# The last normed tile's splits, the place of M4 and the last pair's down weights in a hybrid decoder layer's FFN

## The chip, the cores and the metric

One Trainium2 chip, one NeuronCore of it. The number that counts is the device time of one execution in microseconds (us), the median of several. All engines are named as the profile names them: PE is the matrix engine, DVE the vector engine, ACT the scalar engine, POOL GpSimd, SP the engine that issues the DMAs here.

## What is computed

One decoder layer on x[1, 1024, 1024] in float32, cut to the lines that matter here:

```python
mod = silu(c) @ w_ada + b_ada                      # shift1, scale1, gate1, shift2, scale2, gate2
h = rmsnorm(x, norm1_w) * (1 + scale1) + shift1
proj = h @ w_in                                    # queries, keys, index heads, retention, gates
y_a = dsa_attention(...) @ w_attn_proj             # top-256 index search, then attention
y_r = (silu(gr) * head_groupnorm(retention)) @ w_ret_proj
merged = sigmoid(ga) * y_a + sigmoid(gb) * y_r
x = x + gate1 * (merged @ w_out)
h2 = rmsnorm(x, norm2_w) * (1 + scale2) + shift2
ffn = (silu(h2 @ w_ffn_gate) * (h2 @ w_ffn_up)) @ w_ffn_down    # 2816 hidden columns
x = x + gate2 * ffn
return rmsnorm(x, final_norm_w)
```

## The kernel before

Every matrix product is made from float32 operands that are split into a high part (ACT rounds it) and a low part (the rest, a subtraction on DVE or POOL). A product of two 128x128 blocks then takes three matmuls: high by high, high by low, low by high.

The change touches the last two of the kernel's stages, the end of the out-projection with it.

**End of the out-projection.** For each of eight tiles of 128 tokens the second half of `merged @ w_out` is added to x, its norm is taken, the normed tile is turned on PE (line 1394), and scaled by ACT (L1400) and DVE (L1404) into `hraw`. The eight tiles go in the order 4, 5, 6, 7, 0, 1, 2, 3. The first four are the token half "2", the last four the token half "1". `put_half1` and `put_rest` make side operands of the scaled tiles with `put_combo`, which is one ACT instruction (L1294, the high part) and one DVE instruction (L1295, the low part): h11 is the first half of the channels of the token half 1, h21 its second half.

**Gate and up projection of the FFN.** The 2816 hidden columns are 11 pairs p = 0 ... 10 of 256; each pair is two streams, one on `w_ffn_gate` and one on `w_ffn_up`, so there are 22 streams. A stream is a 2x2 block product (token halves and channel halves against channel halves and column halves) made in seven block products instead of eight: `M1` to `M7`. The side operands of the seven are made once: h11 for M1, h21 for M2, h22 for M4, S1 for M5, S2 for M6, S4 for M3, S3 for M7 (`split_combo` makes S2, S4 and S3, ACT L1519 and DVE L1520). The other operand of a product, its factor, is a sum of blocks of the stream's weights (DVE L800, L806, L807; M1, M2 and M3 need no sum), split by `split_block` into `fhi` (ACT L761) and `flo` (L762; DVE for the first products, POOL afterwards, by `fenv.lo_engine`). There are five buffers for fhi and flo each. A product is 12 matmuls of 128x128 by 128x512: four blocks of k, each with L838 (high, high), L840 (high, low side) and L842 (low factor, high side). Products add up in two PSUM tiles of a stream: M1, M6, M7 and M4 in its tile `ya`, M5 and M3 in its tile `yb`, M2 in a `yb` of its own. Between them ACT copies (L818) and DVE adds (L821) take partial sums out of these into `c11`, `c12`, `c21`, `c22`; DVE adds and multiplies (L1448) and ACT silus (L1445) finish them. `finish_tasks(p)` puts the pair's seven left operands of the down product on a list: DVE sums, then stores to `act_d` in DRAM by `act_store`, then the loading of down weights (`down_load`, into the tile `dw`) and their sums (`down_sums`, DVE L1502) and the store of these to `dw_d` in DRAM. Two of these tasks are taken off after each product.

**Order.** The list `seq` names (stream, product) in the order in which the program issues them: the first two streams product by product, then stream after stream in `ORDER = M1, M5, M6, M3, M7, M2, M4`. A scheduler then places each engine's instructions; `turns_after(ins, other)` asks it to keep one instruction behind another, without a wait of its own. Every engine works through its own queue in order.

**Down product.** The same seven products, each summed over the 11 pairs: `down_slot` loads a 128x512 block from `act_d`, `dw_d` or `w_ffn_down` into a ring of eight (`draw`), and splits it (ACT L1603; DVE or POOL L1604) into a `dslot`. The products go M1, M5, M6, M3, M7, M4 and M2; PE runs them at L1621 to L1623. At the end the final norm is applied, with `fnorm`.

Of the kernel before, what the change touches and what calls it, by code (L numbers as in the profile page):

```python
# [43 lines left out]
def tile_hybrid_layer(ctx: ExitStack, tc: tile.TileContext, x, c, w_ada, b_ada, norm1_w, w_in,  # L44
# [715 lines left out]
    def split_block(src, hi, lo, eng=None):  # L760
        ins = nc.scalar.activation(hi, src, AF.Copy)  # L761
        (eng or nc.gpsimd).tensor_sub(lo, src, f32(hi))  # L762
        return ins

    class Stream:
# [28 lines left out]
        def factor(self, m):  # L794
# [18 lines left out]
            self.split = split_block(src, hi, lo, self.env.lo_engine)  # L813
# [70 lines left out]
    class GateEnv:  # L884
# [423 lines left out]
    def put_half1(o):  # L1308

        h11, h21, h12, s1 = parts_of(o)  # L1310
        put_combo("h11", o, h11)
        nc.vector.tensor_sub(s1, s1, h11)

    def put_rest(o):

        h11, h21, h12, s2 = parts_of(o)
        put_combo("h21", o, h21)
        nc.vector.tensor_sub(h21, h21, s2)

# [28 lines left out]
    for hf in range(2):  # L1348
# [16 lines left out]
        for n, t in enumerate(order):  # L1365
# [130 lines left out]
    def down_sums(p):  # L1496
# [16 lines left out]
        todo.insert(4, lambda: nc.sync.dma_start(out=dw_d[p], in_=dws[p]))  # L1513

    def split_combo(name, srcs):
        alloc_combo(name)
        for k in range(4):
            hi, lo = (c[:, k, :] for c in combo[name])
            nc.scalar.activation(hi, srcs[:, k, :], AF.Copy)  # L1519
            nc.vector.tensor_sub(lo, srcs[:, k, :], f32(hi))  # L1520
# [13 lines left out]
    for st in flow[:2]:  # L1534
        st.prepare("M1")
        turns_after(scaled[3], st.split)
    s3 = ffn.tile([P, 4, H], F32, name="s3", tag="dw")
    held2 = const.tile([P, 2, H], F32, name="held2", tag="gate")

    for st, after in zip(flow, (None, {0: 2}, {2: 3}, {0: 3})):  # L1540
        st.product("M5", after)
        if st.p == 0:
            turns_after(scaled[3], st.copied)
    split_combo("S2", hraw[1][:, 1])
# [3 lines left out]

    def behind(i):
        st, m = seq[i]  # L1550
        if i == 0:
            for k in range(4):
                nc.vector.tensor_sub(s3[:, k, :], hraw[0][:, 0, k, :], hraw[1][:, 0, k, :])
        if i == 1:
# [3 lines left out]
        if i == 8:  # L1558
            fenv.lo_engine = nc.gpsimd
        if i == 9:  # L1560
# [30 lines left out]
    fnorm = ffn.tile([P, 4, H], F32, name="fnorm", tag="dw")[:, 0:2, :].rearrange("p a n -> p (a n)")  # L1591
    nc.sync.dma_start(out=fnorm, in_=final_norm_w.rearrange("(o d) -> o d", o=1).partition_broadcast(P))
# [163 lines left out]
```

## Time and profile before

| what | us |
|---|---|
| time, median of 3 runs | 1771.59 (1771.57 to 1774.38) |
| the profiled execution's own time | 1770.31 |
| its span, first to last instruction | 1768.4 |
| PE busy in the span | 1696.3 (96%) |
| DVE, POOL, ACT busy | 1216.7 (69%), 882.4 (50%), 757.2 (43%) |
| mean granted clock of PE | 0.991 |

The span is the time from the first to the last instruction on the core. A full granted clock is 1.00. Of PE's busy time the page says that matmuls are pipelined, so the start-to-start distance of neighbouring matmuls says more than their durations.

### The profile page before, as it was taken

Reading aid. Unit: us, or ns where it says so; the run is one execution under the profiler, and the core shown is the slowest. Engines: PE = TensorE matmul, PEld = TensorE weight load, DVE = VectorE, ACT = ScalarE, POOL = GpSimd, SP = SyncE. Lnnn points to the kernel's source line nnn. Section 1 sums busy time; section 2 is a strip of 40 time slices with the busy share of each in tenths; the row PEclk is TensorE's granted clock in tenths of the full one; section 3 lists DMA queues with packets and bytes.
Section 4 is the critical chain, followed back from the end, with each engine's and each line's share of the span. In section 5 each row is a group of like instructions: output and inputs, shape, how many; then the busy total and the mean of one; then the engine's idle time right before and its main releaser. Section 6 shows DMA issues by size and latency. Waiting matters only on the chain. (4 is left out here: it accounts for less than half of the span.)

```text
span 1768.4 us, 24625 instructions
## 1 busy us (share of the span) xinstructions
PE 1696.3 (96%) x8266; PEld 1393.6 (79%) x8266; DVE 1216.7 (69%) x2099; ACT 757.2 (43%) x1469; POOL 882.4 (50%) x873
## 2 busy tenths in 40 slices
PE   5899989999999999999999999899999999999998
PEld 4797768888878887788777888688787778787887
DVE  7529793888998687574675747865756565686665
ACT  3625533333544444430676146533333333444444
POOL 3563275683544678430355631054544445556564
PEclk9999999999999999999999999999999999999999
DMA  9535452512333355964843720134444444597762
GB/s 276 161 99 169 149 162 62 149 39 57 117 90 131 112 172 176 291 182 146 196 116 136 244 98 1 54 107 165 158 156 160 137 150 143 203 320 247 209 183 107
DMA packets 182654, 266.48 MB, mean 151 GB/s; under 512 B 13872, under 2 KB 111616, under 8 KB 180096
## 3 DMA queue, kind: packets, MB, share of 16 engines
q1 hardware_dynamic: 182528, 264.91, 48.1%
q8 instruction: 65, 1.06, 0.3%
q14 instruction: 61, 0.50, 0.1%
HBM read 195.39 MB, written 69.47 MB: 150 GB/s over the span
## 5 line engine op out<-in xcount | busy, mean ns | idle before, releaser
L80 POOL TENSOR_TENSOR wlo<-wraw,whi 128x512 fp32r<-128x512 f32 (+2 forms) x116 | 147.0, 1279 | 105.3 <-ACT whi L77 86.3
L463 DVE TENSOR_SCALAR_CACHE_REDUCE eq<-score,cand 128x384 uint8<-128x384 f32 (+2 forms) x192 | 180.5, 940 | 3.6
L762 POOL TENSOR_TENSOR flo<-tmp,fhi 128x512 fp32r<-128x512 f32 x79 | 107.1, 1356 | 139.7 <-ACT fhi L761 111.8
L121 PE MATMUL mm<-whi,hT_hi 128*128 128x512 f32 (+1 forms) x432 | 159.8, 376 | 3.8 <-ACT qk L650 1.8
L124 PE MATMUL mm<-whi,hT_lo 128*128 128x512 f32 (+1 forms) x432 | 161.5, 376 | 0.0
L123 PE MATMUL mm<-wlo,hT_hi 128*128 128x512 f32 (+1 forms) x432 | 160.3, 374 | 0.0
L838 PE MATMUL ya<-hc,fhi 128*128 128x512 f32 x344 | 134.6, 392 | 2.3 <-DVE c L821 1.4
L1604 DVE TENSOR_TENSOR dslot<-draw,dslot 128x512 fp32r<-128x512 f32 x88 | 94.7, 1107 | 58.4 <-ACT dslot L1603 54.2
L1603 ACT ACTIVATE dslot<-draw 128x512 fp32r<-128x512 f32 x154 | 90.4, 626 | 102.9 <-DMA draw<-dw_d 23.4
L840 PE MATMUL ya<-hc,fhi 128*128 128x512 f32 x344 | 133.9, 389 | 0.0
L842 PE MATMUL ya<-hc,flo 128*128 128x512 f32 x344 | 132.4, 389 | 0.0
L1604 POOL TENSOR_TENSOR dslot<-draw,dslot 128x512 fp32r<-128x512 f32 x66 | 98.0, 1498 | 65.4 <-ACT dslot L1603 61.7
L762 POOL TENSOR_TENSOR flo<-raws,fhi 128x512 fp32r<-128x512 f32 x60 | 82.1, 1369 | 92.7 <-ACT fhi L761 64.2
L77 ACT ACTIVATE whi<-wraw 128x512 fp32r<-128x512 f32 (+2 forms) x116 | 67.0, 590 | 112.0 <-DMA wraw<-in_w_in_dram 46.4
L840 PE MATMUL yb<-hc,fhi 128*128 128x512 f32 x256 | 100.6, 393 | 6.1 <-DVE hc L1295 6.1
L842 PE MATMUL yb<-hc,flo 128*128 128x512 f32 x256 | 100.7, 394 | 3.2 <-POOL flo L762 3.2
L761 ACT ACTIVATE fhi<-tmp 128x512 fp32r<-128x512 f32 x84 | 53.0, 631 | 113.1 <-PE ya L840 61.4
L838 PE MATMUL yb<-hc,fhi 128*128 128x512 f32 x256 | 100.6, 394 | 0.6 <-DVE c L821 0.4
L121 PEld LDWEIGHTS mm<-whi,hT_hi 128*128 128x128 f32 x432 | 80.9, 188 | 16.0 <-ACT qk L650 2.2
L1144 POOL TENSOR_SCALAR sx<-sx,mx 128x128 f32<-128x128 f32 (+7 forms) x64 | 47.8, 752 | 88.0 <-DVE mx L1143 65.1
L124 PEld LDWEIGHTS mm<-whi,hT_lo 128*128 128x128 f32 x432 | 81.3, 189 | 12.7 <-issue 0.5
L807 DVE TENSOR_TENSOR tmp<-raws 128x512 f32<-128x512 f32 x40 | 39.5, 989 | 74.3 <-POOL flo L762 74.3
(410 smaller groups left out, 4950.9 us busy)
## 6 DMA issues: line engine op xcount, KB each, us to landing
draw<-act_d SPq DMA_DIRECT2D x77, 256.0 KB
mw<-in_w_ada_dram SPq DMA_DIRECT2D x32, 512.0 KB
act_d<-c SPq DMA_DIRECT2D x64, 256.0 KB
raw<-in_w_in_dram SPq DMA_DIRECT2D x26, 512.0 KB
raws<-in_w_ffn_gate_dram SPq DMA_DIRECT2D x24, 512.0 KB
raws<-in_w_ffn_up_dram SPq DMA_DIRECT2D x24, 512.0 KB
dw<-in_w_ffn_down_dram SPq DMA_DIRECT2D x22, 512.0 KB
dw_d<-dw SPq DMA_DIRECT2D x11, 1024.0 KB
```

The costliest lines, as they stand in the source:

```text
L77: ins = nc.scalar.activation(hi[:, :n], raw[:, :n], AF.Copy)
L80: nc.gpsimd.tensor_sub(lo[:, :n], raw[:, :n], f32(hi[:, :n]))
L121: ins = nc.tensor.matmul(ps, lhsT=ahi, rhs=whi[:, :n], start=(i == 0), stop=False)
L123: nc.tensor.matmul(ps, lhsT=ahi, rhs=wlo[:, :n], start=False, stop=False)
L124: nc.tensor.matmul(ps, lhsT=alo, rhs=whi[:, :n], start=False, stop=(i == last))
L463: ins = [nc.vector.tensor_scalar(eq[:, :sc.shape[1]], sc, thr[j], None, op0=op, op1=ALU.add, accum_out=cnt[:, j:j + 1]) for j, sc in enume ...
L762: (eng or nc.gpsimd).tensor_sub(lo, src, f32(hi))
L838: mm = nc.tensor.matmul(ps, lhsT=whi[:, k, :], rhs=hhi[:, k, :], start=own and k == 0, stop=False, skip_group_check=True)
L840: nc.tensor.matmul(ps, lhsT=whi[:, k, :], rhs=hlo[:, k, :], start=False, stop=False, skip_group_check=True)
L842: nc.tensor.matmul(ps, lhsT=wlo[:, k, :], rhs=hhi[:, k, :], start=False, stop=k == 3, skip_group_check=True)
L1603: nc.scalar.activation(slot[:, 0], raw, AF.Copy)
L1604: lo_eng.tensor_sub(slot[:, 1], raw, f32(slot[:, 0]))
```

## The change

It has three parts.

1. The FFN's first side sums, factor sums and splits on ACT and DVE are put behind the splits of h11 and h21 of the last normed tile. `split_block` and `put_combo` return the instructions to name, and `FfnEnv.in_turn` asks for the order with `turns_after`. The low parts of the first two streams' M1 factors are kept ahead. The matmuls of the fourth stream's early M5 wait one k-block later for the last tile's turning on PE, and S4 and S3's sums are issued a product later.
2. From the third stream on, M4 of a stream changes places with M1 of the next one in `seq`.
3. The last pair (p = 10) keeps its seven left operands and its sums of down weights in their tiles; `down_slot(..., here=True)` splits them from there, without the stores, the loads and the `draw` buffer. `fnorm` moves from the `dw` tag to two `quad` tiles, with the squares' scratch tile in a third.

```diff
     def split_block(src, hi, lo, eng=None):
         ins = nc.scalar.activation(hi, src, AF.Copy)
-        (eng or nc.gpsimd).tensor_sub(lo, src, f32(hi))
-        return ins
+        return ins, (eng or nc.gpsimd).tensor_sub(lo, src, f32(hi))
...
-                    nc.vector.tensor_sub(src, b["12"], b["11"])
-                nc.vector.tensor_sub(src, b[x], b[y] if y else self.t1)
+                    self.env.in_turn(None, nc.vector.tensor_sub(src, b["12"], b["11"]))
+                self.env.in_turn(None, nc.vector.tensor_sub(src, b[x], b[y] if y else self.t1))
...
-            self.split = split_block(src, hi, lo, self.env.lo_engine)
+            self.split, self.lo = split_block(src, hi, lo, self.env.lo_engine)
+            self.env.in_turn(self.split, self.lo)
...
-            (put_half2 if th else put_half1)(o)
+            last_h11 = (put_half2 if th else put_half1)(o)
     alloc_combo("h21")
     for i in range(4):
-        put_rest(i * P)
+        last_h21 = put_rest(i * P)
...
     class FfnEnv:
         lo_engine = nc.vector
+        behind = []
+
+        def in_turn(self, scalar, vector):
+
+            for hi, lo in self.behind:
+                if scalar is not None:
+                    turns_after(scalar, hi)
+                turns_after(vector, lo)
...
-            todo.append(lambda m=m, t=t: act_store(p, m, t))
+            if p < NP - 1:
+                todo.append(lambda m=m, t=t: act_store(p, m, t))
+            else:
+                last_act[m] = t
...
-        todo.insert(4, lambda: nc.sync.dma_start(out=dw_d[p], in_=dws[p]))
+        if p < NP - 1:
+            todo.insert(4, lambda: nc.sync.dma_start(out=dw_d[p], in_=dws[p]))
...
         turns_after(scaled[3], st.split)
+        turns_after(last_h11[1], st.lo)
+    fenv.behind = [last_h11, last_h21]
...
-    for st, after in zip(flow, (None, {0: 2}, {2: 3}, {0: 3})):
+    for st, after in zip(flow, (None, {0: 2}, {2: 3}, {1: 3})):
...
+    for i in [i for i, (st, m) in enumerate(seq[:-1]) if m == "M4" and i >= n_first]:
+        seq[i:i + 2] = seq[i + 1], seq[i]
+
     def behind(i):
         st, m = seq[i]
-        if i == 0:
+        if i == 1:
+            fenv.behind += [(f.split, f.lo) for f in flow[:2]]
             for k in range(4):
-                nc.vector.tensor_sub(s3[:, k, :], hraw[0][:, 0, k, :], hraw[1][:, 0, k, :])
-        if i == 1:
+                fenv.in_turn(None, nc.vector.tensor_sub(s3[:, k, :], hraw[0][:, 0, k, :], hraw[1][:, 0, k, :]))
             split_combo("S4", hraw[0][:, 1])
...
         if i == 8:
             fenv.lo_engine = nc.gpsimd
+            fenv.behind = []
...
-    def down_slot(src, lo_eng, scale=None):
+    def down_slot(src, lo_eng, scale=None, here=False):
+
         n = n_slot[0]
         n_slot[0] += 1
-        raw, slot = raw_ring[:, n % 8, :], slot_rings[n // 4 % 6][:, n % 4]
-        nc.sync.dma_start(out=raw, in_=src)
+        raw, slot = src if here else raw_ring[:, n % 8, :], slot_rings[n // 4 % 6][:, n % 4]
+        if not here:
+            nc.sync.dma_start(out=raw, in_=src)
...
-        s = down_slot(act_d[p][:, ACT_AT[m], :], nc.vector)
+        here = p == NP - 1
+        s = down_slot(last_act[m] if here else act_d[p][:, ACT_AT[m], :], nc.vector, here=here)
         if m in DW_AT:
+            if here:
+                return s, down_slot(dws[p][:, DW_AT[m], :], nc.gpsimd, here=True)
```

**The first place** is DVE's queue at the last normed tile. In the names, `hc_10739` is the side operand h11, `hc_10963` h21, `hc_11077` S2, `hc_11128` S4; `hraw2` and `hraw5` hold the scaled tiles; `flo_11008` and `flo_11014` are the low factors of M1 of the first two streams, `flo_11087` and its neighbour those of M2, `flo_11140` that of M6 of the first. Before, behind the last tile's four scalings (L1404):

```order
L1404 TENSOR_SCALAR hraw2_10422<-ty_10951,modr_1397 128x128 x4
...
L762 TENSOR_TENSOR flo_11008<-raws_10191,fhi_11007 128x512
L762 TENSOR_TENSOR flo_11014<-raws_10191,fhi_11013 128x512
...
L1553 TENSOR_TENSOR s3_11017<-hraw2_10422,hraw5_10423 128x512
L762 TENSOR_TENSOR flo_11087<-raws_10191,fhi_11086 128x512
L762 TENSOR_TENSOR flo_11110<-raws_10191,fhi_11109 128x512
L1295 TENSOR_TENSOR hc_10963<-hraw2_10422,hc_10963 128x4x128
L1295 TENSOR_TENSOR hc_10739<-hraw2_10422,hc_10739 128x4x128
L762 TENSOR_TENSOR flo_11140<-tmp_11003,fhi_11139 128x512
```

And now, in one piece up to the low parts of S2:

```order
L1409 TENSOR_SCALAR hraw2_10422<-ty_10951,modr_1397 128x128 x4
L1322 TENSOR_TENSOR hraw2_10422<-hraw2_10422,hraw5_10423 128x4x128
L762 TENSOR_TENSOR flo_11008<-raws_10191,fhi_11007 128x512
L762 TENSOR_TENSOR flo_11014<-raws_10191,fhi_11013 128x512
L1298 TENSOR_TENSOR hc_10963<-hraw2_10422,hc_10963 128x4x128
L1298 TENSOR_TENSOR hc_10739<-hraw2_10422,hc_10739 128x4x128
```

and further down in the same queue, where now the low factor of M6 stands:

```order
L1538 TENSOR_TENSOR hc_11077<-hraw5_10423,hc_11077 128x512 x3
L806 TENSOR_TENSOR tmp_11003<-raws_10191,tmp_11003 128x512
L806 TENSOR_TENSOR tmp_11004<-raws_10191,tmp_11004 128x512
L821 TENSOR_TENSOR c11_11103<-c11_11103,yb_11148 128x512
L821 TENSOR_TENSOR c11_11122<-c11_11122,yb_11174 128x512
L1538 TENSOR_TENSOR hc_11128<-hraw2_10422,hc_11128 128x512 x4
L762 TENSOR_TENSOR flo_11140<-tmp_11003,fhi_11139 128x512
```

Before, 15 instructions stood between the last scaling and the two splits, and the low factor of M6 came right behind them; now three stand ahead of the splits, and 24 between the splits and M6's low factor (among them four each for S2, for the sums `s3` and for S4).

**The second place** is ACT's queue in the steady part, where PE's M6 of one stream waits for ACT to copy M1's sum out of its `ya`. Before, the copy of it (`c11_12063`) stands behind the silu of `c21_12040`, which reads the sum of the other stream's M4:

```order
L761 ACTIVATE fhi_12091<-tmp_12089 128x512
L761 ACTIVATE fhi_12109<-raws_10191 128x512
L1445 ACTIVATE c21_12040<-ya_11898 128x512
L818 ACTIVATE c11_12063<-ya_12050 128x512
L761 ACTIVATE fhi_12128<-tmp_12044 128x512
```

Now the same copy (`c11_12039` there) stands two places higher:

```order
L761 ACTIVATE fhi_12091<-tmp_12089 128x512
L818 ACTIVATE c11_12039<-ya_12026 128x512
L761 ACTIVATE fhi_12109<-raws_10191 128x512
L1458 ACTIVATE c21_12063<-ya_11876 128x512
L761 ACTIVATE fhi_12127<-raws_10191 128x512
```

It moved ahead of the split for M2 and of the silu, and the split of the next stream's M1 factor (`fhi_12127`) now comes where that of M4 was.

**The third place** is the way of the last pair's down weight for M5. Before, on SP, the load of the weights (L1490), the store of their sums to `dw_d10` and the load from there:

```order
L1490 DMA dw_14262<-in_w_ffn_down_dram 128x1024 x2
...
L1513 DMA dw_d10_11002<-dw_14262 128x2048
L1600 DMA draw_14272<-dw_d2_10994 128x512
L1600 DMA draw_14272<-act_d7_10988 128x512
L1600 DMA draw_14272<-act_d8_10989 128x512
L1600 DMA draw_14272<-dw_d8_11000 128x512
L1600 DMA draw_14272<-act_d9_10990 128x512
L1600 DMA draw_14272<-dw_d9_11001 128x512
L1592 DMA fnorm_14279<-in_final_norm_w_dram 128x1024
L1600 DMA draw_14272<-dw_d10_11002 128x512
```

Now, on ACT, where `c11_14104` is the tile with the last pair's left operand of M5 and `dw_14255` the tile with the sums:

```order
L1633 ACTIVATE dslot_14269<-c11_14104 128x512
L1633 ACTIVATE dslot_14269<-draw_14264 128x512
L1633 ACTIVATE dslot_14270<-draw_14264 128x512
L1633 ACTIVATE dslot_14269<-draw_14264 128x512
L1633 ACTIVATE dslot_14270<-draw_14264 128x512
L1633 ACTIVATE dslot_14269<-dw_14255 128x512
```

The store and the load are gone from SP's queue, and the split reads the tile that DVE sums into.

## Rows read from the trace of the kernel before

**Rows 1.** The page: span, and part 1 (busy us, share, instructions of an engine).

```profile
span 1768.4 us, 24625 instructions
...
PE 1696.3 (96%) x8266; PEld 1393.6 (79%) x8266; DVE 1216.7 (69%) x2099; ACT 757.2 (43%) x1469; POOL 882.4 (50%) x873
```

**Rows 2.** Waits of PE, 1000 to 1768 us: who for whom: sum, times, longest.

```profile
PE yb L840 <- DVE hc L1295: 6.1, 1, 6.1
PE yb L842 <- POOL flo L762: 3.2, 4, 0.8
PE yb L1621 <- ACT dslot L1603: 3.0, 1, 3.0
PE ya L838 <- DVE c L821: 1.4, 4, 0.4
PE ty L1394 <- DVE xn L1391: 1.0, 1, 1.0
PE ya L838 <- ACT c L818: 0.9, 4, 0.2
```

**Rows 3.** Timeline of PE, last normed tile (start, us, what, idle before).

```profile
1113.07 1.06 PE L1394 MATMUL ty<-ident,xn 128*128 128x128 f32 x8 [0.99 <-DVE xn L1391]
...
1118.54 0.61 PE L838 MATMUL ya<-hc,fhi 128*128 128x512 f32 x2
1125.22 0.79 PE L840 MATMUL yb<-hc,fhi 128*128 128x512 f32 x1 [6.07 <-DVE hc L1295]
...
1126.24 0.63 PE L838 MATMUL yb<-hc,fhi 128*128 128x512 f32 x1
1126.66 0.63 PE L840 MATMUL yb<-hc,fhi 128*128 128x512 f32 x1
```

**Rows 4.** PE by stretch: us, busy (matmuls), granted clock, DMA share, GB/s.

```profile
1112.00:1113.00 1.00, 0.08 (x1) 1.00 0.00 0
1123.00:1129.00 6.00, 3.78 (x9) 0.50 0.02 7
1129.00:1142.00 13.00, 13.00 (x58) 1.00 0.06 21
1350.00:1450.00 100.00, 98.23 (x428) 1.00 0.48 165
1607.40:1614.00 6.60, 6.54 (x16) 0.52 0.63 200
```

**Rows 5.** Timeline of DVE at the last normed tile.

```profile
1114.17 1.36 DVE L1404 TENSOR_SCALAR hraw<-ty,modr 128x128 f32<-128x128 f32 x4 [0.25 <-PE ty L1394]
...
1124.48 1.28 DVE L1295 TENSOR_TENSOR hc<-hraw,hc 128x512 fp32r<-128x512 f32 x2
...
1140.41 1.29 DVE L762 TENSOR_TENSOR flo<-raws,fhi 128x512 fp32r<-128x512 f32 x2
```

**Rows 6.** Timeline of PE in the steady streams.

```profile
1255.94 0.50 PE L838 MATMUL ya<-hc,fhi 128*128 128x512 f32 x1 [0.24 <-ACT c L818]
...
1334.71 0.50 PE L838 MATMUL ya<-hc,fhi 128*128 128x512 f32 x1 [0.24 <-ACT c L818]
```

**Rows 7.** Timelines in the steady streams, two rows of DVE, then one of POOL.

```profile
1269.99 1.80 DVE L800 TENSOR_TENSOR tmp<-raws,tmp 128x512 f32<-128x512 f32 x1
1271.72 0.68 DVE L821 TENSOR_TENSOR c<-c,ya 128x512 f32<-128x512 f32 x1
...
1294.44 1.27 POOL L762 TENSOR_TENSOR flo<-raws,fhi 128x512 fp32r<-128x512 f32 x1 [3.49 <-PE ya L842]
```

**Rows 8.** The chain that ended last, 1585 to 1620 us: start, us, what.

```profile
1591.91 1.68 DVE dw L1502
1593.61 4.93 DMA dw_d<-dw
...
1599.03 7.73 DMA draw<-dw_d
...
1607.46 1.22 PE yb L1621 x2
```

More of the change, by code (lines that the diff above doesn't have):

```diff
@@ L907, in quad, with in_turn @@
             return quads[(self.n_q - 1) % len(quads)]
+        def in_turn(self, *_):
+            pass
         def store(self, st, dst, src):
@@ L1310, in put_half1 @@
         h11, h21, h12, s1 = parts_of(o)
-        put_combo("h11", o, h11)
-        nc.vector.tensor_sub(s1, s1, h11)
+        ins = put_combo("h11", o, h11)
+        turns_after(nc.vector.tensor_sub(s1, s1, h11), ins[1])
+        return ins
     def put_rest(o):
         h11, h21, h12, s2 = parts_of(o)
-        put_combo("h21", o, h21)
+        ins = put_combo("h21", o, h21)
         nc.vector.tensor_sub(h21, h21, s2)
+        return ins
     raws = []
@@ L1465, in tile_hybrid_layer @@
     todo = []
+    last_act = {}
     def finish_tasks(p):
@@ L1543, in tile_hybrid_layer @@
             turns_after(scaled[3], st.copied)
+        else:
+            turns_after(st.copied, last_h11[0])
     split_combo("S2", hraw[1][:, 1])
@@ L1590, in tile_hybrid_layer @@
     n_slot = [0]
-    fnorm = ffn.tile([P, 4, H], F32, name="fnorm", tag="dw")[:, 0:2, :].rearrange("p a n -> p (a n)")
-    nc.sync.dma_start(out=fnorm, in_=final_norm_w.rearrange("(o d) -> o d", o=1).partition_broadcast(P))
-    nc.gpsimd.tensor_scalar(fnorm, fnorm, float(D ** 0.5), 1.0, op0=ALU.mult, op1=ALU.mult)
+    fnorm = [quad_tile("fnorm") for _ in range(2)]
+    for hf, fn in enumerate(fnorm):
+        nc.sync.dma_start(out=fn, in_=final_norm_w[hf * H:(hf + 1) * H].rearrange("(o d) -> o d", o=1)
+                          .partition_broadcast(P))
+        nc.gpsimd.tensor_scalar(fn, fn, float(D ** 0.5), 1.0, op0=ALU.mult, op1=ALU.mult)
     xo_all = slab_tile(7, [P, 8, H], F32, "xo")
-    def down_slot(src, lo_eng, scale=None):
+    def down_slot(src, lo_eng, scale=None, here=False):
         n = n_slot[0]
         n_slot[0] += 1
-        raw, slot = raw_ring[:, n % 8, :], slot_rings[n // 4 % 6][:, n % 4]
-        nc.sync.dma_start(out=raw, in_=src)
+        raw, slot = src if here else raw_ring[:, n % 8, :], slot_rings[n // 4 % 6][:, n % 4]
+        if not here:
+            nc.sync.dma_start(out=raw, in_=src)
         if scale is not None:
@@ L1636, in square @@
             ss3[t] = const.tile([P, 16], F32, name="ss3", bufs=4)
-        sq = ffn.tile([P, H], BF16, name="sqh", tag="quad", bufs=10)
+        if not squares:
+            squares.append(ffn.tile([P, H], BF16, name="sqh", tag="quad", bufs=10))
+        sq = squares[0]
         nc.scalar.activation(sq[:, :c1 - c0], x1[t][:, c0:c1], AF.Square, accum_out=ss3[t][:, i:i + 1])
@@ L1649, in final_norm @@
         nc.sync.dma_start(out=out[t * P:(t + 1) * P, H:], in_=xo[1])
-        nc.vector.scalar_tensor_tensor(xo[0], x1[t][:, :H], rs, fnorm[:, :H], op0=ALU.mult, op1=ALU.mult)
+        nc.vector.scalar_tensor_tensor(xo[0], x1[t][:, :H], rs, fnorm[0], op0=ALU.mult, op1=ALU.mult)
         nc.sync.dma_start(out=out[t * P:(t + 1) * P, :H], in_=xo[0])
@@ L1654, in second_half @@
         square(t, 0, H, 2 * H)
-        nc.gpsimd.tensor_mul(xo_all[:, (2 * t + 1) % 8, :], x1[t][:, H:], fnorm[:, H:])
+        nc.gpsimd.tensor_mul(xo_all[:, (2 * t + 1) % 8, :], x1[t][:, H:], fnorm[1])
     banks = {"A": [ps_a() for _ in range(4)], "B": [ps_b(), ps_b(), ps_ty(), ps_ty()]}
```

10 lines of the change are left out of this document (5 added, 5 removed).

## The prediction

> **What bounds the kernel now.** I read the page first: PE is busy 1696.3 of 1768.4 us [rows 1]. Only time in which PE stands still, or runs at half clock, can be won without taking matmuls away, and the change takes none away. So I read PE's waits over the stages that it touches, then the granted clock there, then the queues of the engines that PE waits for. The waits show three things of the change's concern [rows 2]. PE waits once, 6.1 us, for DVE's low parts of h11 and h21; twelve times, 5.5 us together, in the steady streams, for POOL's `flo`, DVE's additions and ACT's copies; and once, 3.0 us, for ACT's `dslot` in the down product. After the first and the last the granted clock is at 0.50 and 0.52, PE's lower level (1.2 GHz), in 1123 to 1129 and 1607.4 to 1614; a matmul then follows the last one after 0.42 to 0.43 us [rows 3, 4]. At full clock (1.00, 2.4 GHz) it is 0.2267 us: 13.00 us hold 57.3 of them (58 begin) [rows 4].
>
> **Part 1, the last tile's splits.** The loss there now: 6.07 us of idle time at 1125.22, nine matmuls at half clock (9 x 0.20 = 1.8 us), and 0.99 us of idle time before the last tile is turned [rows 3, 4]; 8.9 us in all, and the upper bound of this part.
>
> The added order costs no instruction. DVE's own work is the point. Between the last scaling (1114.17, 1.36 us) and the splits (1124.48) stand 15 instructions, in the 9.0 us that are left between: about 0.60 us each from start to start [rows 5]. Now three stand there. The last turning comes at best some 0.5 us earlier (33 instead of 34 matmuls of M5 ahead of it, and its tile is normed earlier, because the out-projection's last matmuls no longer stand behind twelve of M5), so I put the scalings' end at 1115.0. Three more instructions and two splits end at 1115.0 + 5 x 0.60 = 1118.0. PE gets M1 from about 1118.1 where it was 1125.22, and the 24 matmuls of M1 and then 24 of M2 run through, to 1118.1 + 46 x 0.2267 = 1128.5 (two were issued before).
>
> But the same DVE work has to be done, and DVE is busy from 1114.17 until 1141.7, 46 instructions with hardly a pause between them [rows 5]. What is late next is M6 of the first stream. Its `flo` stood right behind the splits; now it is the 30th instruction behind the scaling, at 1115.0 + 30 x 0.60 = 1133.0. Two of these are additions that wait for M2's end, at 1126 and 1128.9, which they reach in time. M6's `fhi` comes at about 1128.9, and two matmuls can go ahead of `flo`. PE so stands still 0.4 + 3.6 us. Behind M6, M4's `flo` needs six more of DVE's instructions (1137.3; four are the low parts of S3). PE's 65th matmul from M1's first on, the one that needs it, ran at 1129.13 + 51 x 0.2277 = 1140.7 before. Now it runs at 1137.3 if the clock stays full, and at 1133.1 + 14 x 0.427 = 1139.1 if it falls as it did behind the 2.96 us of idle time at 1607.46. Gain 3.4 or 1.6 us. I take 2.0, since both long stalls of these stages, 6.07 and 2.96 us, were followed by half clock [rows 2 to 4]. Bounds: 8.9, if M6's `flo` comes in time, and -2.4 (a rival below).
>
> Here a rule weighs against the change. The row shows a 1.0 us pause (1112 to 1113) and the steady streams' pauses of up to 0.8 us with the clock at 1.00 [rows 2, 4]: short pauses cost their own length and no more. The Trainium skill, page "TensorE: Matmul & The Clock Gate", section "A second HAM failure mode: psum-queue depth-cycling", says otherwise: an engine that idles briefly, but often, between groups of matmuls can have its clock swing between both levels. By it the three pauses in a row that I expect (0.4, 3.6, up to 1.0 us) would keep the clock down until the last of them is over; by the row the part is worth 2.0, by the rule it costs 2.4.
>
> **Part 2, M4 behind the next M1.** The streams repeat every four: the same wait comes at 1255.94 and 1334.71, 78.77 us apart [rows 6]. A period is 28 products of 12 matmuls, 336 x 0.2267 = 76.2 us. So 2.6 us are lost per period, to three pauses (0.24, 0.35 and 0.80 us [rows 2, 6]) and the slower matmuls beside them, and 10.4 us in the four periods that the twelve waits make up. That is the upper bound; the lower one is 0.
>
> Each pause has its cause in the order. ACT's copy of M1's sum (M6 writes there next) stands behind a silu that needs M4. The addition to `c22`, which frees M4's tile, stands at 1271.72 behind a factor sum of 1.80 us, with sums of down weights ahead of both [rows 7]. And POOL's `flo` for M2 waits 3.49 us for the last matmul of M5, which PE runs only after M4 (the row names the last of M4, just ahead of it), and M2 comes right behind [rows 7]. In the changed order the copy stands ahead of the silu; the addition to `c22` comes ahead of the sums of down weights; and 12 matmuls of M6 (2.7 us) lie between M5's last one and M2. `flo` needs 1.27 us on POOL, about 2.5 us with ACT's `fhi` ahead of it, against 2.7 + 0.45 us until M2's third matmul. I found no product with less room than this one in the new order. Value taken: 8.5 of 10.4, because room of 0.6 us may not do everywhere, and because the pattern at its beginning and end differs.
>
> **Part 3, the last pair.** Now: DVE's last sums end at 1593.6, the store takes 4.93 us, the load 7.73, and PE starts at 1607.46 after 2.96 us of idle time [rows 2, 8]; then 16 matmuls lie in 6.54 us, 16 x 0.2 = 3.2 us more than at full clock [rows 4]. Removed are one store of 1 MB, four loads from it, seven stores and seven loads of 256 KB. The split from the tile can start at 1593.6 and needs ACT's 0.64 and POOL's 1.3 to 1.5 us; even with another such pair ahead of it, it is done by 1598, and PE comes there at 1604.4. So 6.0 of 6.2 us are won. The bounds are 0, if a different `dslot` is as late (the next loads come one place earlier in SP's queue, so nothing points there), and 6.2. The `fnorm` load is two of half the size, read only at the end: nothing.
>
> **Sum.** 2.0 + 8.5 + 6.0 = 16.5 us. The profiled execution took 1770.3 us (1.9 us outside its span), 1.3 less than the median of 1771.6. The three parts are the same in both, so I take it from the median: 1755.1, say 1755.
>
> **The rivals.**
> - *M6's split is in time* (DVE faster than 0.60 us an instruction, or its additions not waited for): part 1 brings 8.9 and the time is 1748. Against it: the 46 instructions before were not faster [rows 5].
> - *The clock stays low across part 1's three pauses*, until 1142: twenty matmuls more at 0.427, 1.6 - 4.0 = -2.4, and 1759.5. For it: half clock after both long stalls [rows 4]. Against it: full clock across short ones [rows 2, 4]. The rule cited above would have it so.
> - *The steady pauses come again elsewhere*, as other products wait behind the new neighbours: part 2 brings 0 and the time is 1763.5. For it: DVE's and POOL's queues are in order, and a sum on DVE next to POOL's work takes up to 1.80 us [rows 7].
> - *The last pair's wait only changes its name*: 1761.
> - *It doesn't move PE's end at all*, each gain given back before the next stage: 1771.6. The order lists speak against it, since PE is the bound everywhere.
> - *Slower*: with four products opened side by side (M2 and M1 run two matmuls early and end behind M7), two of the five `fhi`/`flo` buffers are bound 24 matmuls (5.4 us) longer, and M5's next split has 5.4 us from the release to its use. If release, ACT and POOL took 7.4 instead of my 2.5 us, each of the ten pairs of streams would lose 2.0 us, 20 in all, and the time would be 1775. It decides from 5.4 us on. Against it: POOL had done 1.3 us after such a release [rows 7].
>
> **How the numbers follow.** Forecast as summed 0.52; M6's split in time 0.12; low clock 0.10; steady pauses come again 0.12; the last pair's wait stays 0.04; no effect 0.06; slower 0.04. 0.2%, about what a measurement of this kernel can tell from none, is 3.5 us. The first five are faster by more than that: 0.90. Same 0.06, slower 0.04. The range goes from 1748 (M6 in time, all else as summed) to 1764 (steady pauses come again), and leaves out the last two cases and parts of others, some 2 in 10.
>
> **What would show it.** Part 1 right: PE's wait for `hc` falls to about 1 us, and a new wait of 3 to 4 us for `flo` by DVE (L762) appears at M6, with half clock behind it. Part 2 right: the waits for POOL's `flo`, DVE's `c` and ACT's `c` are gone from 1150 to 1540, and the pattern repeats every 38.1 us (two streams, 168 matmuls). Part 3 right: no wait for `dslot`, and a clock of 1.00 around 1600. Wrong: waits of more than 0.3 us for `flo` in each pair of streams, or a wait for `dslot` of 2 us and more.

## The result, and the profile after

The changed kernel takes 1755.08 us (median of 4 runs, 1754.88 to 1759.13); the kernel before, run beside it on the same chip, takes 1771.74. The ratio is 0.9908, with an interval of 0.9891 to 0.9925. So the time fell by 16.7 us, 0.9%. One run of this study, the eighth of E5, fell in the chip's slower state (1904.08 us) and is left out.

The profiled execution is the slowest of the four, 1759.13 us, with a span of 1756.9. Its stages ahead of the change account for that: the first turning of the second half of the out-projection, at 1067.90 us before, starts at 1072.83. The code up to there is the same in both kernels, and the granted clock is lower there (0.95, 0.98 and 0.97 in the first three hundreds of microseconds, where it was 0.98, 1.00 and 0.98). Wherever a time of after is set against one of before, these 4.93 us are taken off first, and the text says "aligned".

The page of the kernel after, the lines that answer to [rows 1]:

```profile
span 1756.9 us, 24623 instructions
...
PE 1694.5 (96%) x8266; PEld 1397.6 (80%) x8266; DVE 1226.4 (70%) x2099; ACT 756.0 (43%) x1469; POOL 888.7 (51%) x874
```

PE does the same 8266 matmuls, and its busy time is nearly the same; the time came out of its pauses. These are PE's waits from 1000 to 1768 us, as in [rows 2]:

```profile
PE ya L838 <- DVE c L821: 2.0, 2, 1.6
PE ya L842 <- DVE flo L762: 1.9, 1, 1.9
PE ya L838 <- ACT fhi L761: 1.7, 1, 1.7
PE ya L840 <- DVE hc L1298: 0.6, 1, 0.6
```

The 6.1 us for `hc` are 0.6. The twelve waits of the steady streams (POOL's `flo`, ACT's `c`, DVE's `c`) are down to two, the wait for `dslot` is gone, and two waits are new: for ACT's `fhi` and DVE's `flo` of one product. Where they are, PE's timeline shows (start, duration, what, and in brackets the idle time before it with its releaser); it answers to [rows 3, 6]:

```profile
1117.51 1.03 PE L1399 MATMUL ty<-ident,xn 128*128 128x128 f32 x8
...
1123.02 0.51 PE L840 MATMUL ya<-hc,fhi 128*128 128x512 f32 x1 [0.59 <-DVE hc L1298]
...
1135.52 0.50 PE L838 MATMUL ya<-hc,fhi 128*128 128x512 f32 x1 [1.74 <-ACT fhi L761]
1135.86 0.40 PE L840 MATMUL ya<-hc,fhi 128*128 128x512 f32 x1
1138.18 0.79 PE L842 MATMUL ya<-hc,flo 128*128 128x512 f32 x1 [1.93 <-DVE flo L762]
1138.78 0.63 PE L838 MATMUL ya<-hc,fhi 128*128 128x512 f32 x1
...
1143.90 0.47 PE L840 MATMUL ya<-hc,fhi 128*128 128x512 f32 x1
1144.21 0.40 PE L842 MATMUL yb<-hc,flo 128*128 128x512 f32 x1
...
1274.37 0.50 PE L838 MATMUL ya<-hc,fhi 128*128 128x512 f32 x1 [0.34 <-DVE c L821]
...
1544.01 0.50 PE L838 MATMUL ya<-hc,fhi 128*128 128x512 f32 x1 [1.65 <-DVE c L821]
```

M1 starts and runs through; the new stall is at M6 of the first stream, and from 1138.18 to 1143.9 the matmuls follow one another in steps of 0.43 us. Between 1274 and 1544 us PE stands still nowhere. The stretches, as in [rows 4] (us, busy and count of PE, of its weight loads, DVE, ACT, POOL, then clock, DMA share, GB/s), say the same of the clock:

```profile
1138.00:1144.00 6.00, 5.82 (x14) 4.56 (x15) 6.00 (x11) 2.79 (x6) 0.00 (x0) 0.50 0.12 44
...
1350.00:1450.00 100.00, 100.00 (x443) 82.88 (x442) 62.72 (x70) 37.30 (x65) 51.51 (x38) 1.00 0.49 169
1600.00:1620.00 20.00, 20.00 (x90) 16.58 (x89) 18.59 (x17) 11.62 (x20) 16.59 (x10) 1.00 0.65 207
```

A hundred microseconds of steady streams hold 443 matmuls instead of 428, with no pause, and around 1600 the clock is 1.00. Two queues tell what PE waits for. First DVE, at the last tile (as [rows 5]) and, 400 us later, at the end of the last stream:

```profile
1118.58 1.37 DVE L1409 TENSOR_SCALAR hraw<-ty,modr 128x128 f32<-128x128 f32 x4
...
1121.67 1.29 DVE L1298 TENSOR_TENSOR hc<-hraw,hc 128x512 fp32r<-128x512 f32 x2
...
1133.83 1.29 DVE L821 TENSOR_TENSOR c<-c,yb 128x512 f32<-128x512 f32 x2
1135.03 2.50 DVE L1538 TENSOR_TENSOR hc<-hraw,hc 128x512 fp32r<-128x512 f32 x4
1137.43 0.70 DVE L762 TENSOR_TENSOR flo<-tmp,fhi 128x512 fp32r<-128x512 f32 x1
...
1539.77 1.78 DVE L1634 TENSOR_TENSOR dslot<-draw,dslot 128x512 fp32r<-128x512 f32 x1
1541.47 0.68 DVE L1461 TENSOR_TENSOR c<-c,c 128x512 f32<-128x512 f32 x1
1542.07 0.68 DVE L1634 TENSOR_TENSOR dslot<-draw,dslot 128x512 fp32r<-128x512 f32 x1
1542.67 0.68 DVE L1519 TENSOR_TENSOR dw<-dw 128x512 f32<-128x512 f32 x1
1543.28 0.68 DVE L821 TENSOR_TENSOR c<-c,ya 128x512 f32<-128x512 f32 x1
```

Then ACT, ahead of M6's `fhi`:

```profile
1132.75 2.19 ACT L1537 ACTIVATE hc<-hraw 128x512 fp32r<-128x512 f32 x4 [3.78 <-DVE hc L1538]
1134.85 0.61 ACT L761 ACTIVATE fhi<-tmp 128x512 fp32r<-128x512 f32 x1
```

On both engines the four parts of S4 (L1537, L1538) stand right ahead of what M6 waits for: 2.19 us on ACT, 2.50 us on DVE. S4 itself is needed only by M3. ACT had stood idle for 3.78 us ahead of S4's parts, until DVE was through with the low parts of S2 (L1538): S4 is written into the memory of `hraw5`, which these read, and on DVE the four sums `s3` (2.49 us) and four factor sums stand ahead of the last of them. So DVE's queue set ACT's time, too.

**Where the time came from.** To give each part its share I cut the program at events of PE. T0 is the first turning of the out-projection's second half. Stretch 1 goes from there to the 113th matmul of the FFN (the 65th from M1's first on, which in after needs M4's `flo`), stretch 2 to the first down matmul into a `yb` tile, and stretch 3 to the last one into a `ya` tile. Part 1 acts in the first, part 2 in the second, part 3 in the third. All kernels of this study, one profile each, in us:

| kernel | T0 | stretch 1 | stretch 2 | stretch 3 | sum of the three |
|---|---|---|---|---|---|
| before | 1067.9 | 72.8 | 434.6 | 186.3 | 693.7 |
| after | 1072.8 | 71.4 | 426.0 | 179.8 | 677.2 |
| after, second profile (E9) | 1074.2 | 71.1 | 426.0 | 179.8 | 676.9 |
| part 1 alone (E1) | 1069.5 | 70.2 | 434.6 | 185.7 | 690.5 |
| part 2 alone (E2) | 1066.8 | 73.9 | 426.0 | 181.6 | 681.5 |
| part 3 alone (E3) | 1070.7 | 72.7 | 435.4 | 179.8 | 687.9 |
| part 3, sums only (E5) | 1070.4 | 72.5 | 434.4 | 179.8 | 686.7 |
| part 3, operands only (E6) | 1068.1 | 73.8 | 435.4 | 180.3 | 689.5 |
| M4 behind M1 in half the places (E7) | 1065.5 | 72.8 | 429.2 | 183.0 | 685.0 |
| after, S4 later (E4) | 1071.6 | 64.4 | 427.2 | 179.8 | 671.4 |
| the same again (E10) | 1074.0 | 64.4 | 427.2 | 179.8 | 671.4 |
| E4, M4 moved in half the places (E11) | 1066.1 | 64.4 | 427.2 | 179.8 | 671.4 |
| after, S4's low parts on POOL (E12) | 1069.4 | 69.2 | 426.1 | 179.8 | 675.1 |
| E4 with two more orders (E8) | 1069.7 | 63.8 | 430.9 | 179.8 | 674.5 |

T0 moves by 8.7 us between profiles of unchanged code, which is half of the whole effect; the stretches behind it, where the code is the same, agree within 1.4 us. Stretch 3 of E2 and E7 is the exception; see there. The three stretches of before and after differ by 1.4, 8.6 and 6.5 us, together 16.5, beside 16.7 between the medians.

### The profile page after: what moved, and what is told of

Same layout as the page of the kernel before. It is cut to its first block, busy times and chain, and to the rows that moved or that the text cites. A ratio compares the mean times of both kernels' runs of the same rounds, so it can differ in the third digit from the quotient of the medians.

```text
span 1756.9 us, 24623 instructions
## 1 busy us (share of the span) xinstructions
PE 1694.5 (96%) x8266; PEld 1397.6 (80%) x8266; DVE 1226.4 (70%) x2099; ACT 756.0 (43%) x1469; POOL 888.7 (51%) x874
## 4 chain that ended last, share of the span: by engine, by line
PE 63%; DVE 4%; DMA 1%; issue 1%; ACT 0%; SPq 0%; POOL 0%; POOLq 0%; DVEq 0%; ACTq 0%
PE ya L838 4%; PE ya L842 4%; PE ya L840 4%; PE yb L840 3%; PE yb L838 3%; PE yb L842 3%; PE ya L1656 2%; PE ya L1655 2%; PE ya L1654 2%; PE pva L1179 2%; PE mm L840 2%; PE mm L842 2%; PE mm L838 2%; PE tra L1158 2%; PE lg L838 1%; PE lg L842 1%
## 5 line engine op out<-in xcount | busy, mean ns | idle before, releaser
L1633 ACT ACTIVATE dslot<-draw 128x512 fp32r<-128x512 f32 x143 | 85.1, 628 | 93.4 <-DMA draw<-act_d 24.9
L762 POOL TENSOR_TENSOR flo<-raws,fhi 128x512 fp32r<-128x512 f32 x60 | 86.0, 1438 | 73.9 <-ACT fhi L761 39.2
L1634 DVE TENSOR_TENSOR dslot<-draw,dslot 128x512 fp32r<-128x512 f32 x81 | 90.6, 1150 | 45.4 <-ACT dslot L1633 45.1
L806 DVE TENSOR_TENSOR tmp<-raws 128x512 f32<-128x512 f32 x40 | 30.7, 768 | 87.5 <-POOL flo L762 87.5
```

The source lines that it names most:

```text
L762: return ins, (eng or nc.gpsimd).tensor_sub(lo, src, f32(hi))
L1633: nc.scalar.activation(slot[:, 0], raw, AF.Copy)
L1634: lo_eng.tensor_sub(slot[:, 1], raw, f32(slot[:, 0]))
```

## The experiments

All of them compute the layer in full, with the same matmuls; only the order of work and the way of the last pair's tiles differ. Times are medians; the ratios are to the kernel before, run beside it.

**E1 to E3: each part alone.** The core of each edit, against the kernel before:

```diff
+        turns_after(last_h11[1], st.lo)
+    fenv.behind = [last_h11, last_h21]
```

for E1,

```diff
+    for i in [i for i, (st, m) in enumerate(seq[:-1]) if m == "M4" and i >= n_first]:
+        seq[i:i + 2] = seq[i + 1], seq[i]
```

for E2, and for E3

```diff
-        s = down_slot(act_d[p][:, ACT_AT[m], :], nc.vector)
+        here = p == NP - 1
+        s = down_slot(last_act[m] if here else act_d[p][:, ACT_AT[m], :], nc.vector, here=here)
```

> Part 1 alone on the kernel before. My theory: the last tile's splits come some 7 us earlier, PE's wait for hc falls to about 0.6 us, and 3.5 to 4 us of waiting appear at M6 of the first stream (its fhi and flo), with half clock behind: 1.5 us gained in all, 1770.2. Rival 1, the stall only changes its place: within 1 us of 1771.7. Rival 2, the stall is gone and part 1 is worth its 8.9 us: 1763. The steady streams' waits and the one for dslot stay as before.

> Part 2 alone on the kernel before. My theory: the waits between 1150 and 1530 us go, 8.5 us gained, 1763.2; the pattern repeats every 38.1 us. Rival 1, the waits come again elsewhere when the other parts are missing: 1768 or more. Rival 2, all 10.4 us are gained: 1761.3. PE's wait for hc at the last normed tile stays at 6.1 us. Open: whether the wait of 1.65 us for DVE's c at the last stream's M4, which the changed kernel has and the one before has not, comes from this part.

> Part 3 alone on the kernel before. My theory: the wait for dslot and the half clock behind it go, 6.2 us, 1765.5. Rival 1: less DMA traffic helps other stages too, more than 7.5 us, below 1764. Rival 2: another dslot is as late, 1770 or more.

| part | time | ratio, interval | before |
|---|---|---|---|
| E1, splits first | 1766.85 (12 runs) | 0.9982, 0.9969 to 0.9995 | 1770.8 |
| E2, M4 behind M1 | 1757.26 (5 runs) | 0.9926, 0.991 to 0.9942 | 1770.8 |
| E3, last pair on chip | 1767.78 (12 runs) | 0.9985, 0.9974 to 0.9997 | 1770.8 |

By the medians the parts bring 4.0, 13.5 and 3.0 us, where 1.5, 8.5 and 6.2 were forecast; by the stretches 3.2, 12.2 and 5.8. In E1 the waits are those of after at the last tile (1.9 for DVE's `flo`, 1.8 for ACT's `fhi`, 0.6 for `hc`) and those of before everywhere else, only that the one for `dslot` is 3.8 us long. In E3 the wait for `dslot` is gone, and a down matmul waits 0.6 us for a product of DVE (L1448) instead. E2 holds two surprises. One is that the new wait of 1.7 us for DVE's `c` is there too, so it belongs to part 2. The other is in stretch 3: it is 4.7 us shorter, though part 2 touches nothing there. The rows of E2's PE timeline, at M1 and in the down product:

```profile
1124.09 0.80 PE L840 MATMUL yb<-hc,fhi 128*128 128x512 f32 x1 [6.08 <-DVE hc L1295]
...
1129.80 0.57 PE L838 MATMUL yb<-hc,fhi 128*128 128x512 f32 x1
1130.21 0.40 PE L840 MATMUL yb<-hc,fhi 128*128 128x512 f32 x1
...
1595.71 0.39 PE L1626 MATMUL ya<-dslot 128*128 128x512 f32 x1
1597.31 0.73 PE L1624 MATMUL yb<-dslot 128*128 128x512 f32 x2 [1.21 <-ACT dslot L1606]
```

and the stretch around the second of these waits:

```profile
1596.00:1600.00 4.00, 2.79 (x13) 2.21 (x13) 2.05 (x2) 2.72 (x5) 3.63 (x3) 1.00 0.58 219
```

The wait for `dslot` is 1.21 us instead of 2.96, and no half clock follows it, where before it did [rows 4]. DVE's sums end 12.3 us ahead of the matmul that needs them (1583.78, and 1596.1), where it was 10.8 (1593.6, and 1604.4). So the parts overlap: by the stretches they bring 21.2 us one by one, and the change brings 16.5. In the change, part 3 takes what part 2 has partly taken already.

**E4 and E10: is S4 what M6 waits for?** S4 is split two products later and the sums `s3` are made four products later, behind the low factors that are needed sooner. Against the kernel after:

```diff
+        if i == 3:
+            fenv.behind += [(f.split, f.lo) for f in flow[:2]]
+            split_combo("S4", hraw[0][:, 1])
+        if i == 5:
             for k in range(4):
                 fenv.in_turn(None, nc.vector.tensor_sub(s3[:, k, :], hraw[0][:, 0, k, :], hraw[1][:, 0, k, :]))
-            split_combo("S4", hraw[0][:, 1])
-        if i == 3:
             split_combo("S3", s3)
```

> The changed kernel with the split of S4 issued two products later, and the sums s3 with their split four and two products later, so that on DVE M6's flo of the first stream comes some 12 instructions (7 us) earlier. My theory: what is left of the stall at M6 (3.7 us of idle time and 14 matmuls at half clock, 2.8 us) goes: 1749, with the clock at 1.00 from 1130 to 1150. Rival 1: DVE's work is only moved, and the stall comes at M3 or M7 (S4 or S3 late): 1753 to 1756. Rival 2: the idle time goes but the clock falls all the same: 1751.5.

> The kernel with S4 and s3 later, on the same chip as the changed kernel. My theory from its first run's trace: 7.0 us less up to M4 of the first stream, 1.1 us given back later (a wait of 0.85 us for DVE's c), so 4 to 6.5 us faster than the changed kernel; the rival, that the difference of the two calls was the chip's: less than 2 us.

E4 takes 1750.96 us (ratio 0.9891, 0.9873 to 0.9908), E10 1751.93 (0.99, 0.9887 to 0.9913). Beside E10 on its chip E9, the change once more, takes 1755.77 (0.9922, 0.991 to 0.9934):

> The changed kernel itself, beside the next three on one chip, to compare with them. 1755.1 if the chip is like the one before it; 16 to 17 us below the kernel before of the same call.

The waits of E4:

```profile
PE ya L838 <- DVE c L821: 2.0, 2, 1.7
PE ya L838 <- DVE c L852: 0.8, 1, 0.8
PE ya L840 <- DVE hc L1298: 0.6, 1, 0.6
```

and the stretch in which after stood still and ran at half clock:

```profile
1130.00:1145.00 15.00, 15.00 (x68) 12.39 (x67) 14.57 (x25) 10.75 (x19) 1.99 (x2) 1.00 0.42 136
```

The forecast of no stall and a full clock holds; the time is 2 us above its 1749. Both waits at M6 are gone, PE runs 15 us without a pause at full clock, and stretch 1 falls from 71.4 to 64.4 us. Of these 7.0 us, 3.7 are the waits (1.74 and 1.93) and 2.8 the fourteen matmuls at half clock (14 x 0.2); the rest is within what the stretch varies by. The delayed sums cost 1.2 us in stretch 2, where PE now waits 0.85 us for a partial sum (L852). So the place of S4 and of the sums `s3` is the cause of the stall at M6; E4 moves both and doesn't tell their shares. By the stretches 5.5 to 5.8 us more were to be had. By the medians beside each other, E9 and E10, it is 3.8 us, just under the 4 to 6.5 that were forecast, and E9 is 14.6 us below the kernel before where 16 to 17 were.

**E12: one of the two queues.** As a control, S4 stays where it is, and only its low parts go to POOL. Against the kernel after:

```diff
+        eng = nc.gpsimd if name == "S4" else nc.vector
...
-                         nc.vector.tensor_sub(lo, srcs[:, k, :], f32(hi)))
+                         eng.tensor_sub(lo, srcs[:, k, :], f32(hi)))
```

> The changed kernel, with the low parts of S4 on POOL in place of DVE. My theory, DVE's work decides: M6's flo comes 4 instructions (2.4 us) earlier, its wait falls from 1.9 us to below 0.7, half clock behind it goes or is short, 1.5 to 4 us gained. Rival: POOL's four subtractions and DVE's hold each other up (DVE's 1.8 in place of 0.6 us beside them, POOL's several us each), M6's flo is no earlier or M3 waits for S4: no gain, or up to 3 us lost.

It takes 1754.85 us (0.9916, 0.9903 to 0.9929). PE's timeline at M6:

```profile
1132.12 0.50 PE L838 MATMUL ya<-hc,fhi 128*128 128x512 f32 x1 [1.77 <-ACT fhi L761]
1132.46 0.40 PE L840 MATMUL ya<-hc,fhi 128*128 128x512 f32 x1
1133.50 0.57 PE L842 MATMUL ya<-hc,flo 128*128 128x512 f32 x1 [0.65 <-DVE flo L762]
1133.87 0.63 PE L838 MATMUL ya<-hc,fhi 128*128 128x512 f32 x1
```

and DVE's instruction ahead of 1133.50:

```profile
1132.10 1.34 DVE L762 TENSOR_TENSOR flo<-tmp,fhi 128x512 fp32r<-128x512 f32 x1 [0.38 <-ACT fhi L761]
```

DVE's share of the stall falls from 1.93 to 0.65 us, so S4's four low parts made at least 1.3 us of it; ACT's share stays (1.74, 1.77), as S4's high parts do. What is left on DVE is no longer S4's turn in the queue: `flo` waits 0.38 us for `fhi`, and takes 1.34 us instead of 0.70 beside POOL, which works on S4's low parts from 1130.07 to 1136.27. To that extent the rival came true. Half clock comes nevertheless (steps of 0.43 from 1133.87 on), and the sum of the stretches falls by 1.8 to 2.1 us only, the median by 0.9 us beside E9.

**E5 and E6: what made the last `dslot` late?** Part 3 keeps two things on chip, and each experiment keeps one of them. The prediction put the wait down to the store and the load of the sums, which E5 takes out and E6 leaves in. The core of E5, against the kernel before:

```diff
         s = down_slot(act_d[p][:, ACT_AT[m], :], nc.vector)
+            if here:
+                return s, down_slot(dws[p][:, DW_AT[m], :], nc.gpsimd, here=True)
```

and of E6:

```diff
+            if p < NP - 1:
+                todo.append(lambda m=m, t=t: act_store(p, m, t))
+            else:
+                last_act[m] = t
```

> Only half of part 3 on the kernel before: the last pair's sums of down weights stay on the chip, its left operands go through DRAM as before. My theory: the wait for dslot hangs on the store and the load of the sums alone (4.93 and 7.73 us in a row), so it goes, and the down product is 6.2 to 6.4 us shorter, as with all of part 3. Rival: the left operands' loads are as late, and 1.5 us or more of the wait stay.

> The other half of part 3 on the kernel before: the left operands of the last pair stay on the chip, the sums go through DRAM. My theory: the wait for dslot stays between 2.3 and 4 us, with half clock behind it; the down product is less than 1 us shorter. Rival: with seven stores and seven loads fewer the store and the load of the sums are so much faster that the wait falls below 1.5 us.

E5 takes 1765.95 us (0.9981, 0.9968 to 0.9994) and has no wait for `dslot`; its stretch 3 is 6.5 us shorter than that of before. But E6, at 1766.53 (0.9978, 0.9969 to 0.9988), has none either, and its stretch 3 is 180.3 us: my theory, by which the wait had to stay in E6, falls. SP's queue in E6 (the load of the last pair's down weights, and the store of their sums):

```profile
1566.74 0.90 SPq L1494 DMA_DIRECT2D dw<-in_w_ffn_down_dram  x2
...
1578.64 0.32 SPq L1517 DMA_DIRECT2D dw_d<-dw  x1
```

and in the kernel before:

```profile
1582.07 0.90 SPq L1490 DMA_DIRECT2D dw<-in_w_ffn_down_dram  x2
...
1593.61 0.32 SPq L1513 DMA_DIRECT2D dw_d<-dw  x1
```

In E6 the weights are loaded 15.3 us earlier, and their sums are stored 15.0 us earlier. `down_load` is ordered behind the last `act_store`, and in E6 the last pair has none. E6 also moves less data, and its expectation names a faster way as the rival. By the semaphores of the two traces it was no faster: from the end of the sums to the landing of the load that waits for their store it took 12.9 us in E6 (1578.6 to 1591.5) and 13.2 in before (1593.6 to 1606.8). In E5 the load is where it was (1582.87), and the shorter way is enough. So the wait was the sum of two things, a load that stood late in SP's queue and a way of sums through DRAM, and it was 2.96 us long; taking away either ends it.

**E7: are the steady waits due to M4's place?** Only the M4s of the streams on `w_ffn_up` change places, against the kernel before:

```diff
+    for i in [i for i, (st, m) in enumerate(seq[:-1]) if m == "M4" and st.u == 1 and i >= n_first]:
+        seq[i:i + 2] = seq[i + 1], seq[i]
```

> Part 2 on the kernel before, but only the M4 of the up streams changes places with the next M1. In PE's order M2 then stands again right behind M5's last matmul (M5:1, M2:2, M1:2, M2:10) once in four streams, with only four matmuls (0.9 us) between where flo needs 1.3 us on POOL. My theory: a wait for POOL's flo of 0.3 to 0.6 us stays, four or five times, at that place and nowhere else; the stretch up to the down product is 5 to 8 us shorter than before. Rival: the wait comes from POOL's load, not from M5's buffer, and is then gone (as in the whole of part 2) or at another place.

It takes 1760.76 us (0.9955, 0.9938 to 0.9972). ACT's waits are gone and POOL's are half, 1.6 us in four (three of 0.26 and one of 0.80), at the place that was foreseen. DVE's four of 0.35 us stay, which was not. Stretch 2 gains 5.4 of 8.6 us. Stretch 3 is 3.3 us shorter, as in E2 without an edit there: the wait for `dslot` is 2.51 us, and no half clock follows it (granted clock 1.00 from 1598 to 1606).

```profile
1599.04 0.73 PE L1624 MATMUL yb<-dslot 128*128 128x512 f32 x2 [2.51 <-ACT dslot L1606]
```

**E11: the other half, with S4 later.** Since E7 leaves DVE's waits, I moved the M4s of the other streams, those on `w_ffn_gate`, alone. Against E4:

```diff
-    for i in [i for i, (st, m) in enumerate(seq[:-1]) if m == "M4" and i >= n_first]:
+    for i in [i for i, (st, m) in enumerate(seq[:-1]) if m == "M4" and st.u == 0 and i >= n_first]:
```

> S4 and s3 later, and only the M4 of the gate streams behind the next M1; PE's order then has M5:1, M6:12, M2:12 and no product split but M5. My theory: what decides is that M6's 12 matmuls lie between M5's last one and M2's, and that the up stream's M4 has 12 of M6 before M2 anyway, so no wait comes back: within 1 us of S4 later alone. Rival: the additions to c22 of the streams that do not change places are late again, five waits of 0.35 us and more, 2 us slower.

It takes 1749.66 us (0.9892, 0.9878 to 0.9907), the lowest median of all, but its stretches are those of E4 and E10 to 0.1 us. So these ten exchanges do all of part 2's work, and the others (E7's) none in addition to them. Neither of the two shows what DVE's own waits depend on, beyond that: E7 has them, E11 only one.

**E8: the two waits that remain in E4.** The sums of down weights are put behind the addition to `c22`, and h21's last low part behind h11's. Against E4:

```diff
+            if c == "22":
+                self.env.added22 = self.env.added
...
+    turns_after(last_h21[1], last_h11[1])
...
+                turns_after(ins, fenv.added22)
```

> The kernel with S4 and s3 later, and two more orders on DVE: a down pair's weight sums behind the addition to c22 (M7's), and the last low part of h21 behind that of h11. My theory: the wait of 1.7 us for DVE's c at the last stream's M4 goes and the one of 0.6 us for the low part of h11 goes: 2.3 us less than with S4 later alone (1751.0), 1748.7. Rival: the wait is then for the next instruction of that queue (a dslot's low part), and 1 us or more of it stays: 1750.

It takes 1753.33 us (0.9903, 0.9889 to 0.9918), more than E4 by the stretches (674.5 and 671.4). The wait for `hc` is gone. The other only changes its name:

```profile
1150.42 0.80 PE L844 MATMUL ya<-hc,flo 128*128 128x512 f32 x1 [3.58 <-POOL flo L762]
...
1544.99 0.50 PE L1661 MATMUL ya<-dslot 128*128 128x512 f32 x1 [1.74 <-DVE c L1464]
```

At 1544.99 a down matmul waits 1.74 us for DVE, where a matmul of M4 waited 1.65. And a new wait of 3.58 us stands at 1150.42, with half clock behind it, for these two subtractions of POOL:

```profile
1140.55 3.23 POOL L762 TENSOR_TENSOR flo<-tmp,fhi 128x512 fp32r<-128x512 f32 x1 [30.91 <-ACT fhi L761]
1143.73 6.63 POOL L762 TENSOR_TENSOR flo<-raws,fhi 128x512 fp32r<-128x512 f32 x1
```

## Why the prediction was right

The forecast was 1755, and the median is 1755.08. The terms were 2.0, 8.5 and 6.0; the stretches show 1.4, 8.6 and 6.5. The agreement is closer than the reasons behind it deserve: one term was 0.6 us too large, the others 0.1 and 0.5 too small, and that they cancel is luck. The same kernel took 1755.77 us in E9.

**Part 1, size.** Aligned, the splits are done and PE goes on at 1118.09 (forecast 1118.0 and 1118.1), M6's `flo` comes at 1133.25 (1133.0), and the matmul at which the gain was counted, the 65th, runs at 1139.28 (1139.1 for half clock). The gain at that matmul is 1.4 us. The other profiles tell how sure that is: without part 1 stretch 1 is 72.5 to 73.9 (six kernels, mean 73.1), with part 1 and S4 in its place 70.2 to 71.4 (three, mean 70.9), so the gain is 2.2 us, give or take a microsecond. Most of the spread comes from the clock. After the same stall of 6.1 us, nine matmuls stood at half clock in before [rows 4], and fourteen in E2 (1124.09 to 1129.80).

**Part 1, cause.** The stall at M6 was forecast as 0.4 us for `fhi` and 3.6 for `flo`; it is 1.74 and 1.93, 3.7 in place of 4.0. The step that failed is "M6's `fhi` comes at about 1128.9": PE went on with it at 1130.59, because it stands on ACT behind S4's four high parts, which the forecast counted on DVE only, and which ACT could begin only behind DVE's low parts of S2. It happened not to matter, because the last of the two decides. E4 shows that S4 and `s3` together make the stall, E12 what S4's low parts make of it on DVE; ACT's share is read from its queue and was not tried by itself. The third pause that was expected, for M4's `flo`, did not come.

**Part 2.** The waits that it was to end are gone from 1150 to 1540, except one of 0.34 us, and 8.6 of 10.4 us are won. A wait of 0.45 us for DVE at 1205.72, which [rows 2] don't list, is gone with them. Of the two reasons that I gave for the missing two, the first (that small room may not do everywhere) is not what happened: from 1275 us on the steady streams have no pause. The second (that the pattern differs at its end) holds: the loss is 1.65 us at the last stream's M4. It waits for the addition to `c` at 1543.28, ahead of which low parts of the down product's first slots and sums of down weights stand on DVE; of the nine instructions from 1532.95 on, four take 1.78 or 1.79 us. There M4 meets work that the steady streams don't have; E8, which moves the sums away, only moves the wait.

**Part 3.** The size holds (6.5 for 6.0; alone 6.5 too). The reason was half of it: the store and load of the sums were named as what made `dslot` late, and E6, which keeps them, has no wait. The load's place in SP's queue is the other half.

**The sum** took the parts as independent. They are not (21.2 us alone, 16.5 together), but the terms were each read as what the wait in question costs, and in the stretches of the whole change they come out that way.

**The rivals.** M6 in time came true only in E4: 1751 there, where the rival gave 1748. The low clock across the pauses did not: at 1135.52, after pauses of 0.59 and 1.74 us, the next step (0.34 us) is still the one that follows a pause at full clock; it falls at 1138.18, and it rises again at 1144.2. By the Trainium skill, page "TensorE: Matmul & The Clock Gate", section "A second HAM failure mode: psum-queue depth-cycling", an engine that idles briefly, but often, between groups of matmuls can have a clock that swings; here pauses of 0.34, 0.59 and 0.85 us, and of 1.21, 1.65 and 2.51 us (E7) when they stood alone, left it at full clock, and a fall came with single pauses of 2.96 us and more, and with two of 0.65 to 1.93 us close to one another. So the trace bears the section out only for the last kind. The steady pauses did not come again elsewhere, the last pair's wait did not change its name, and the product with less room, which was to make it slower, shows in no wait.

## What to carry to other kernels

When a wait is moved by an order, list on every engine, not only on the one that waits now, what stands between the new place and the next product; here it was the operands of two later products, on two engines at once, and moving them brought 5.5 to 5.8 us more by the stretches. A transfer can be late because it is long or because it is issued late, and only an experiment that leaves the way as it is and moves the start tells the two apart. Where unchanged stages vary by as much as the effect, cut the program at events that both kernels share and compare stretch by stretch.

## What the hardware showed that was not expected

**POOL's subtraction beside DVE.** A subtraction of 128x512 takes POOL 1.27 us in the steady streams [rows 7], but 3.23 and 6.63 us in E8. DVE ran without a pause then. Most of its instructions there read both operands from SBUF; the additions at 1142.54 and 1149.15 read one, `ya` or `yb`, from PSUM:

```profile
1142.54 1.28 DVE L854 TENSOR_TENSOR c<-c,ya 128x512 f32<-128x512 f32 x2
1143.73 0.68 DVE L805 TENSOR_TENSOR tmp<-raws 128x512 f32<-128x512 f32 x1
1144.34 1.29 DVE L1543 TENSOR_TENSOR hc<-s,hc 128x512 fp32r<-128x512 f32 x2
...
1149.15 1.28 DVE L821 TENSOR_TENSOR c<-c,yb 128x512 f32<-128x512 f32 x2
1150.35 0.69 DVE L806 TENSOR_TENSOR tmp<-raws,tmp 128x512 f32<-128x512 f32 x1
```

The Trainium skill, page "SBUF — State Buffer", section "SBUF: two separate sides", says that a DVE instruction with two operands in SBUF and a GpSimd instruction that reads SBUF exclude one another, each for the length of the instruction. The trace agrees that they hinder each other, but POOL's second subtraction was held up over nine such instructions of DVE, not one. Both subtractions ended (1143.78 and 1150.36) together with a pair of the additions that read PSUM, and such a pair takes 1.28 us, as long as a subtraction of POOL's alone: that fits the section, but it is read from two places only. In the other direction a single DVE instruction takes 1.78 us instead of 0.68, as at 1539.77, beside POOL's low parts of the down product. That the two share a port was not tried by itself.

**How long the clock stays low.** The same stall of 6.1 us was followed by eight matmuls at half clock in E5, nine in before and fourteen in E2 and E6, in the same code; the same two pauses at M6 (1.74 to 1.77 and 1.93 us) by fourteen in after and eight in E1, where five matmuls at full clock came first. After 1.77 and 0.65 us with two matmuls between them (E12) the clock fell; after 1.65 us alone (1544.01 in after) and 2.51 us alone (E7) it did not, and after 2.96 us [rows 4] it did.
